# Attention products and first scores issued later, unequal gate jobs between head pairs, and memory tokens turned by VectorE and DRAM

## The chip, the cores and the metric

The kernel runs on one core of a Trainium2 chip. The metric is device time in microseconds (us), the median of several executions; lower is better. TensorE (PE) multiplies matrices and writes PSUM; VectorE (DVE), ScalarE (ACT) and GpSimd (POOL) work on tiles in SBUF and PSUM; SyncE (SP) issues DMAs, and so do ScalarE and GpSimd from their own queues.

## The reference

One layer of a streaming encoder on 512 tokens of 1024 channels in float32, with 256 memory tokens. The residual stream is normalized and fed to four parallel mixers: A, differential attention with 4 heads; F, forgetting attention with 8 heads of 64; C, a convolution module; D, a short gated convolution. Each mixer's output is projected, weighted by a gate that is itself a product of the normalized tokens, summed, and projected. Then come a cross-attention into the memory tokens and a gated feed-forward part.

```python
h = _rms_norm(x, norm_mix_pre[l])
(a_q, a_k, a_v, f_q, f_k, f_v, f_g, c_u, s_x, s_b, s_c) = jnp.split(h @ w_in[l], cuts, axis=-1)
ya = _diff_attention(...)       # softmax(q1 k1) - lam * softmax(q2 k2), chunk-causal, times v
yf = _forgetting_attention(...) # softmax(q k + c_q - c_k), causal, times v
proj = jnp.einsum('bsnc,ncd->bsnd', jnp.stack([ya, yf, yc, ys], axis=2), w_branch[l])
gates = jax.nn.sigmoid(h @ w_gate[l] + b_gate[l]).reshape(B, S, N_BRANCH, D)
x = x + _rms_norm(jnp.sum(gates * proj, axis=2) @ w_out[l], norm_mix_post[l])
m = _rms_norm(mem, norm_mem[l])
xk, xv = jnp.split(m @ w_xkv[l], 2, axis=-1)   # cross-attention's keys and values
```

## The kernel before

**Arithmetic.** Each float32 product is made of three matmuls: both operands are split into a rounded high part (a cast by ScalarE) and a rest (a subtraction by VectorE), and high x high, low x high and high x low are summed in PSUM (`split` L152 to L156, `split_weights` with the casts on L190 and L191, `matmul` L231). A projection of 128 output channels over 512 tokens is 24 matmuls of 512 columns, called a job below.

**The order of work.** `mixer_jobs` (L1143) yields the jobs of TensorE one after the other: the mixers' projections, the gates' products and the branches' products. `run_blocks` (L203) runs them and loads weights three jobs ahead. Between jobs, `bg.tick()` steps the background tasks (`Background`, L47 to L80): generators that emit the attention's scores, softmax, turning and value products. Each yields an estimated cost and a wait; a task goes on only when an estimated clock, which `matmul` and `transpose` advance, has passed the wait, and while a credit of 0.7 of that clock remains. Two tasks at most are stepped at once. A scheduler then places the emitted instructions in each engine's queue; `tc.issue_after(x)` asks it to place an instruction behind x.

**Attention.** The four heads of A (`a_task`, L860) are queued by `qk_jobs` (L769) between gate jobs of branch c, and the four pairs of heads of F (`f_task`, L1016) between gate jobs of branch a: `mixer_jobs` yields the query and key projections of pair 0, and then, for pairs 1 to 3, the pair's projections and four jobs of the generator `ga` (L1179, L1180). When a pair's keys are projected they are evacuated from PSUM into the tile `qk` (L790 to L792), and its task is queued. A task makes four groups of scores, of 128, 256, 384 and 512 keys, with softmax. The probabilities must be turned (keys on partitions) before they multiply v. There are two ways:

- "far" heads (h < 3) and pairs (p < 3): VectorE turns 32 by 32 squares (`turn_squares` L819), `put` (L822) writes the tile to DRAM from ScalarE's queue, `get` (L831) reads it back in the turned order, and `split_in_place` (L835) casts (L839) and subtracts.
- the last head and the last pair: TensorE transposes through PSUM (`to_keys_major` L804, transposes on L238), and `split` casts and subtracts.

`values` (L842) multiplies with v in two halves, after step 5 and step 7 of the far tasks (3 and 5 of the last). Accumulators of the values are emptied on L1094 and L1095 for F. PSUM banks have the tags mm, av, sc and tr, two of each.

**The memory tokens.** `mem_task` (L1238) is a background task beside the last gate's jobs (branch f): it loads two tiles of 128 memory tokens, normalizes them (`normed` L280), and `to_channels` (L292) has TensorE transpose each (8 transposes), ScalarE cast twice and VectorE subtract twice into `ns.mt`, which the products of `kx_jobs` and `vx_jobs` read after the mixers' output projection.

Of the kernel before, what the change touches and what calls it, by code (L numbers as in the profile page):

```python
# [25 lines left out]
P = 128  # L26
# [57 lines left out]
def hybrid_layer(ctx: ExitStack, tc: tile.TileContext, a: dict, out: bass.AP):  # L84
# [114 lines left out]
        return w[k0 * P:(k0 + nk) * P, c0:c0 + n].rearrange("(k p) c -> p k c", p=P), [P, nk, n]  # L199

    bg = Background(0.7, 2)

    def run_blocks(jobs, ahead=3):  # L203

# [24 lines left out]
            bg.tick()  # L229

    def matmul(ps, lhs, rhs, start, stop):  # L231
        PE.matmul(ps, lhs, rhs, start=start, stop=stop)  # L232
        bg.clock += max(int(math.prod(rhs.shape[1:])), 256) * 0.00042

    turns = []
# [56 lines left out]
    def to_channels(y_t, act, t):  # L292

        sl = slice(t * P, (t + 1) * P)
        for half in range(2):
            ps = bank("tr")
            ks = slice(half * 4, half * 4 + 4)
            for k in range(4):
                transpose(ps[:, k * P:(k + 1) * P], y_t[:, (half * 4 + k) * P:(half * 4 + k + 1) * P])
            split(ps.rearrange("p (k c) -> p k c", k=4), act[0][:, ks, sl], act[1][:, ks, sl])  # L300
# [516 lines left out]
        evacuations[:] = [ins.ins]  # L817

    def turn_squares(dst, src):  # L819
        V.transpose(dst.rearrange("p (b t i) -> p b t i", b=4, i=32), src.rearrange("p (t j b) -> p b t j", b=4, j=32))  # L820

    def put(e, w):  # L822
        d = dram.tile([2, P * S], F32, tag="turned", name="turned", bufs=6)[:e.shape[1], :P * w]
# [36 lines left out]
    def a_task(h, qk, v):  # L860
        es, pt, av = {}, None, None
        far = h < 3
        for step in range(8 if far else 6):
            if step in ((5, 7) if far else (3, 5)):
                if av is None:
                    av = bank("av")
                vh, vl = (x[:, :, h * P:(h + 1) * P] for x in v[0])
                values(av, lambda kt: ((vh[:, kt], 0), (vh[:, kt], 1), (vl[:, kt], 0)), pt, step // 2 - (2 if far else 1))
            cost = 0.0
            if far:  # L870
                for qt in SPLITS.get(step, ()):
                    split_in_place(qt + 1, pt, qt % 2)
                    cost += 0.1 + 0.15 * qt
                for qt in GETS.get(step, ()):
                    if qt % 2 == 0:
                        pt = pt_tiles()
                    get(es.pop(qt)[:, 0], qt + 1, pt, qt % 2)
            elif 1 <= step <= 4:
                if step in (1, 3):
                    pt = pt_tiles()  # L880
                to_keys_major(es.pop(step - 1)[:, 0], step, pt, (step - 1) % 2)
                cost += 0.1 + 0.15 * step
            if step < 4:
                qt, w = step, (step + 1) * P
                e = es[qt] = e4()
                st = m1p.tile([P, 8], F32, tag="st8", name="st8", bufs=4)
                for c in range(2):
                    ps = bank("sc")
                    scores(ps, qk, c, qt * P, w)
                    V.tensor_tensor_reduce(e[:, c, :w], ps[:, :w], mask_a[:, S - w:], scale=1.0,  # L890
                                           scalar=-3.0e38, op0=ALU.add, op1=ALU.max,
                                           accum_out=st[:, c:c + 1])
                V.tensor_scalar(st[:, 2:4], st[:, 0:2], -HD ** -0.5, None, ALU.mult)
                for c in range(2):
                    A.activation(e[:, c, :w], e[:, c, :w], AF.Exp, bias=st[:, 2 + c:3 + c],
                                 scale=HD ** -0.5, accum_out=st[:, 4 + c:5 + c])
                V.reciprocal(st[:, 6:8], st[:, 4:6])
                V.tensor_scalar(st[:, 7:8], st[:, 7:8], lam, None, ALU.mult)
                A.activation(e[:, 1, :w], e[:, 1, :w], AF.Copy, scale=st[:, 7:8])
                V.scalar_tensor_tensor(e[:, 0, :w], e[:, 0, :w], st[:, 6:7], e[:, 1, :w], ALU.mult,  # L900
                                       ALU.subtract)
                cost += 0.6 + 0.0035 * w
                if far:
                    turn_squares(e[:, 1, :w], e[:, 0, :w])
                    es[qt] = put(e[:, 1:], w)
                    cost += 0.0015 * w
            if step == (7 if far else 5):
                e = e4()
                A.copy(e[:, 0], av)
            yield cost, 4.0 if far else 3.5  # L910

        ps = bank("tr")
        for t in range(NT):
            transpose(ps[:, t * P:(t + 1) * P], e[:, 0, t * P:(t + 1) * P])
        A.activation(e[:, 1], ps, AF.Square, scale=1.0 / math.sqrt(P))
        ms = m1p.tile([P, NT], F32, tag="ms4", name="ms4", bufs=2)
        V.tensor_reduce(ms, e[:, 1].rearrange("p (t c) -> p t c", t=NT), AX.X, ALU.add)
        r = rstd_of(m1p, [ms], NT)
        V.tensor_tensor(e[:, 0].rearrange("p (t c) -> p t c", t=NT),
                        ps.rearrange("p (t c) -> p t c", t=NT),  # L920
                        r.unsqueeze(2).to_broadcast([P, NT, P]), ALU.mult)
        yield 1.5, 3.5
        ps2 = bank("tr")
        for t in range(NT):
            transpose(ps2[:, t * P:(t + 1) * P], e[:, 0, t * P:(t + 1) * P])
        if "a" not in y:
            y["a"] = (y8b(), y8b())
        split(ps2, y["a"][0][:, h], y["a"][1][:, h], half["dn"])
        yield 0.6, 0.0
# [86 lines left out]
    def f_task(p, qk, v):  # L1016
# [5 lines left out]
        for j in range(2):  # L1022
            t = m1p.tile([P, S], F32, tag="ck", name="ck", bufs=2)
            G.dma_start(t, crows[2 * p + j:2 * p + j + 1, :].rearrange("a s -> (a s)").partition_broadcast(P))
            ck.append(t)
        yield 0.0, 2.0
        es, pts, av = {}, None, None
        for step in range(8 if far else 6):
            if step in ((5, 7) if far else (3, 5)):
                if av is None:  # L1030
                    av = [bank("av"), bank("av")]
                for j in range(2):
                    hl = v[0][:, :, 2 * p + j]
                    values(av[j], lambda kt: ((hl[:, kt], 0), (hl[:, kt], 1)), pts[j], step // 2 - (2 if far else 1))
            while step == (2 if far else 1) and f_steps[p - 1] < (8 if p - 1 < 3 else 6):
                yield 0.0, 0.5
            f_steps[p] = step + 1
# [19 lines left out]
            if step < 4:  # L1057
# [24 lines left out]
                if far:  # L1082
# [2 lines left out]
                        turn_squares(turned[:, j, :w], e[:, j, :w])  # L1085
                    es[qt] = put(turned, w)
                    cost += 0.003 * w
            yield cost, 4.5
        if "f" not in y:
            y["f"] = (y8(), y8())  # L1090

# [51 lines left out]
    def mixer_jobs():  # L1143
        yield from c_jobs()
        yield then(lambda: bg.add(lam_task(), "lam"))
        yield from d_jobs()
        yield then(lambda: bg.add(conv_norm_task(), "conv"))
        wide = m1p.tile([P, NT, D], F32, tag="v", name="wide")
        free = iter([wide[:, i] for i in (0, 1, 2, 3) * 2])
        ns.out_sums = out_sums = Sums(w_out, NK // 2, lambda: next(free), SP, "out_sums")  # L1150
        steps = {5: (out_sums.load, 0), 6: (out_sums.load, 1), 9: (out_sums.add, 0), 10: (out_sums.store, 0),
                 11: (out_sums.add, 1)}
        for i, job in enumerate(gate_blocks(3, "d")):
            yield job
            if i in steps:
                yield then(lambda f=steps[i]: f[0](f[1]))
        yield then(lambda: y.pop("d"))
        vj = v_jobs(O_AV, va)
        yield then(lambda: (out_sums.store(1), out_sums.load(2), out_sums.load(3)) and None)
        for f, q in ((out_sums.add, 2), (out_sums.add, 3)):  # L1160
            yield next(vj)
            yield then(lambda f=f, q=q: f(q))
            yield then(lambda q=q: out_sums.store(q))
        yield from vj
        yield share(False)
        gc = gate_blocks(2, "c")
        for h, n in enumerate((0, 2, 4, 6)):
            yield from qk_jobs(O_AQ, O_AK, h, lambda qk, h=h: bg.add(a_task(h, qk, va), "a"))
            if n:
                yield then(lambda: bg.drain("conv"))  # L1170
            for _ in range(n):
                yield next(gc)
        yield then(lambda: bg.drain("a"))
        yield from vf_jobs(vf)
        yield from kv_blocks(0)
        ga = gate_blocks(0, "a")
        for p in range(1, 4):
            yield from kv_blocks(p)
            for _ in range(4):  # L1179
                yield next(ga)  # L1180
        yield then(lambda: bg.drain("f"))

# [55 lines left out]
    def mem_task():  # L1238
        for t in range(2):
            m_t = stage("s1", "m_t")  # L1240
            G.dma_start(m_t, mem_d[t * P:(t + 1) * P, :])
            y_t = normed(ns.xm, m_t, [ns.gain], stage("s2", "mn"))
            if t == 0:
                space(ns.xm, "gap8", 96)
            yield 1.3, 8.0
            to_channels(y_t, ns.mt, t)
            yield 1.2, 0.0

    def kx_jobs():
# [577 lines left out]
```

## Time and profile before

| | before |
|---|---|
| median of 3 executions | 1061.24 us (1059.8 to 1061.26) |
| the profiled execution's own time | 1061.52 us |
| its span in the profile | 1059.7 us |
| TensorE busy | 1045.3 us, 99% |
| VectorE busy | 806.2 us, 76% |
| ScalarE busy | 499.7 us, 47% |
| GpSimd busy | 144.7 us, 14% |
| DMA | 164.37 MB, 155 GB/s mean |

All times in the profile are microseconds from the start of the span. A row of the timeline has the start, the duration, the engine, the line, the operation and its operands, and how many instructions it stands for; in square brackets stand the idle time before it and what ended that. Records of matmuls overlap: their starts are what counts. `ps_mm`, `ps_av`, `ps_sc` and `ps_tr` are PSUM banks by tag; `wh` and `wl` are the parts of a weight tile, `pth` and `ptl` of turned probabilities, `mth` and `mtl` of turned memory tokens. A row of the waits has the waiting group, the releaser, the total, how many times, and the longest. The attention of A lies at about 200 to 410 us, F's at 375 to 530, the last gate with the memory tokens at 505 to 575.

### The profile page before, as it was taken

Reading aid. Unit: us, or ns where it says so; the run is one execution under the profiler, and the core shown is the slowest. Engines: PE = TensorE matmul, PEld = TensorE weight load, DVE = VectorE, ACT = ScalarE, POOL = GpSimd, SP = SyncE. Lnnn points to the kernel's source line nnn. Section 1 sums busy time; section 2 is a strip of 40 time slices with the busy share of each in tenths; the row PEclk is TensorE's granted clock in tenths of the full one; section 3 lists DMA queues with packets and bytes.
Section 4 is the critical chain, followed back from the end, with each engine's and each line's share of the span. In section 5 each row is a group of like instructions: output and inputs, shape, how many; then the busy total and the mean of one; then the engine's idle time right before and its main releaser. Section 6 shows DMA issues by size and latency. Waiting matters only on the chain.

```text
span 1059.7 us, 14521 instructions
## 1 busy us (share of the span) xinstructions
PE 1045.3 (99%) x5279; PEld 886.9 (84%) x5279; DVE 806.2 (76%) x1277; ACT 499.7 (47%) x820; POOL 144.7 (14%) x246
## 2 busy tenths in 40 slices
PE   9999999999999999999999999999999999999997
PEld 7888888888888987887878899999888888888886
DVE  6999997568677368787676888886768677667796
ACT  5322222367555355644543665654333333445672
POOL 4000000000000014322110031031111211111001
PEclk9999999999999999999999999999999999999999
DMA  7954333324333245565335743226576676725662
GB/s 260 314 159 96 108 89 100 99 83 141 115 103 108 56 124 173 170 189 145 100 113 177 268 137 119 81 79 193 185 247 214 215 230 213 232 80 179 211 217 79
DMA packets 186109, 164.37 MB, mean 155 GB/s; under 512 B 20352, under 2 KB 158061, under 8 KB 186038
## 3 DMA queue, kind: packets, MB, share of 16 engines
q1 hardware_dynamic: 152995, 119.91, 37.4%
q10 hardware_dynamic: 30482, 35.01, 10.0%
q0 software_dynamic: 2560, 8.54, 2.5%
q8 instruction: 41, 0.67, 0.3%
q14 instruction: 31, 0.25, 0.1%
HBM read 139.69 MB, written 23.74 MB: 154 GB/s over the span
## 4 chain that ended last, share of the span: by engine, by line
PE 89%; issue 4%; DVE 4%; DMA 2%; ACT 1%; POOL 0%; ACTq 0%; SPq 0%; POOLq 0%; DVEq 0%
PE ps_mm L232 46%; PE ps_av L232 29%; PE ps_sc L232 7%; PE ps_tr L232 4%; PE ps_tr L238 2%; DVE wl L191 1%; DMA e<-in_w_in 1%; PE ps_mm L450 1%; PE ps_av L450 1%; DVE e L820 0%; DVE e L1071 0%; ACT e L1076 0%; DMA ck<-crows 0%; DVE e L890 0%; DVE qk L792 0%
## 5 line engine op out<-in xcount | busy, mean ns | idle before, releaser
L190 ACT CAST wh<-wr 128x1024 fp32r<-128x1024 f32 (+1 forms) x140 | 146.7, 1049 | 271.1 <-PE ps_mm L232 154.2
L191 DVE TENSOR_TENSOR wl<-wr,wh 128x1024 fp32r<-128x1024 f32 (+1 forms) x140 | 175.6, 1255 | 104.9 <-ACT wh L190 104.8
L232 PE MATMUL ps_mm<-hth,wh 128*128 128x512 f32 (+1 forms) x616 | 231.0, 381 | 1.0 <-DVE qk L792 0.9
L232 PE MATMUL ps_mm<-htl,wh 128*128 128x512 f32 (+1 forms) x616 | 229.7, 379 | 0.0
L232 PE MATMUL ps_mm<-hth,wl 128*128 128x512 f32 (+1 forms) x616 | 229.4, 379 | 0.0
L232 PEld LDWEIGHTS ps_mm<-hth,wh 128*128 128x128 f32 x616 | 114.3, 188 | 22.4 <-PE ps_sc L232 1.4
L232 PEld LDWEIGHTS ps_mm<-hth,wl 128*128 128x128 f32 x616 | 113.9, 188 | 21.5
L232 PEld LDWEIGHTS ps_mm<-htl,wh 128*128 128x128 f32 x616 | 114.2, 188 | 20.3
L232 PE MATMUL ps_av<-htl,wh 128*128 128x512 f32 (+1 forms) x328 | 122.6, 374 | 0.0
L232 PE MATMUL ps_av<-hth,wh 128*128 128x512 f32 (+1 forms) x328 | 122.5, 374 | 0.0
L232 PE MATMUL ps_av<-hth,wl 128*128 128x512 f32 (+1 forms) x328 | 122.5, 374 | 0.0
L682 DVE SCALAR_TENSOR_TENSOR y<-y,par,y 128x508 f32<-128x508 f32 (+29 forms) x120 | 83.1, 736 | 0.1
L232 PEld LDWEIGHTS ps_av<-hth,wl 128*128 128x128 f32 x328 | 61.7, 188 | 11.0
L232 PEld LDWEIGHTS ps_av<-htl,wh 128*128 128x128 f32 x328 | 61.5, 188 | 10.9
L232 PEld LDWEIGHTS ps_av<-hth,wh 128*128 128x128 f32 x328 | 61.6, 188 | 10.7
L1618 DVE TENSOR_TENSOR wl<-dw,wh 128x1024 fp32r<-128x1024 f32 x32 | 40.1, 1258 | 15.0 <-ACT wh L1617 14.8
L1617 ACT CAST wh<-dw 128x1024 fp32r<-128x1024 f32 x32 | 33.5, 1052 | 22.4 <-PE ps_tr L232 7.9
L1565 ACT ACTIVATE th<-c 128x512 f32<-128x512 f32 x22 | 13.9, 632 | 48.9 <-DVE c L612 48.9
L1065 POOL TENSOR_SCALAR fbias<-ck,cq 128x128 f32<-128x128 f32 (+3 forms) x32 | 22.9, 722 | 78.0 <-DVE st L1071 72.5
L612 DVE SCALAR_TENSOR_TENSOR c<-ps_mm,par,c 128x510 f32<-128x510 f32 (+1 forms) x44 | 32.7, 744 | 0.7
L232 PE MATMUL ps_mm<-y8b,wh 128*128 128x512 f32 x96 | 30.9, 402 | 0.8 <-DVE ge L1124 0.8
L232 PE MATMUL ps_mm<-y,wh 128*128 128x512 f32 x96 | 30.5, 396 | 0.2 <-DVE ge L1124 0.2
(479 smaller groups left out, 2091.8 us busy)
## 6 DMA issues: line engine op xcount, KB each, us to landing
wr<-in_w_up SPq DMA_DIRECT2D x44, 512.0 KB
wr<-in_w_in SPq DMA_DIRECT2D x38, 512.0 KB
wr<-in_w_gate SPq DMA_DIRECT2D x32, 512.0 KB
wp<-in_w_down ACTq DMA_DIRECT2D x22, 512.0 KB
sums<-wp ACTq DMA_DIRECT2D x22, 512.0 KB
dw<-sums SPq DMA_DIRECT2D x44, 256.0 KB
wr<-in_w_branch SPq DMA_DIRECT2D x16, 512.0 KB
wide<-in_w_out SPq DMA_DIRECT2D x12, 512.0 KB
```

What stands on the lines that cost most here:

```text
L190: order(A.copy(hi, raw[:, :n]))
L191: low.tensor_tensor(lo, raw[:, :n], hi.bitcast(F32), ALU.subtract)
L232: PE.matmul(ps, lhs, rhs, start=start, stop=stop)
L238: turns.append(PE.transpose(ps, x, ident[:n, :n]).ins)
L450: keep(PE.matmul(banks[c][:, :S // 2], w[p == 1][:, k, c * P:(c + 1) * P], ht[p == 2][:, i * 4 + k, :S // 2], start=(i, p, k) == (0, 0, 0) ...
L612: ins = V.scalar_tensor_tensor(dst[:, s:], src[:, :S - s], w(k), dst[:, s:], ALU.mult, ALU.add)
L682: ins = V.scalar_tensor_tensor(dst[:, s:], src[:, :S - s], pc("conv_dw", k * 4 + j), dst[:, s:], ALU.mult, ALU.add)
L1065: G.tensor_scalar(bias[:, :w], ck[j][:, :w], -1.0, cq[:, qt, head:head + 1], ALU.mult, ALU.add)
L1565: A.activation(th, c[:, 0], AF.Silu)
L1617: A.copy(hi, x)
L1618: V.tensor_tensor(lo, x, hi.bitcast(F32), ALU.subtract)
```

## The change

- `matmul` keeps its latest instruction in `steps_of`. The value products of far heads and pairs are placed behind the latest matmul emitted before them.
- `a_task` begins with a wait of 3.0; `f_task`'s first wait is 5.0 instead of 2.0. The wait between step 5 of far tasks, which issues the last reads from DRAM, and step 6, which splits them, is 6.0 instead of 4.0 in A and 6.5 instead of 4.5 in F.
- Between the pairs of F stand 3, 4 and 5 jobs of branch a's gate instead of 4, 4 and 4.
- `mem_task` turns the normalized tokens as the far heads do: two stream transposes on VectorE for each tile, a write of the tile to DRAM and four reads from it on ScalarE's queue, then one cast and one subtraction over 1024 columns. The 16 transposes on TensorE and their casts and subtractions are gone.

```diff
     def matmul(ps, lhs, rhs, start, stop):
-        PE.matmul(ps, lhs, rhs, start=start, stop=stop)
+        steps_of[:] = [PE.matmul(ps, lhs, rhs, start=start, stop=stop).ins]
...
     def turn_squares(dst, src):
-        V.transpose(dst.rearrange("p (b t i) -> p b t i", b=4, i=32), src.rearrange("p (t j b) -> p b t j", b=4, j=32))
+        if len(dst.shape) == 2:
+            dst = dst.rearrange("p (b t i) -> p b t i", b=4, i=32)
+        V.transpose(dst, src.rearrange("p (t j b) -> p b t j", b=4, j=32))
...
     def a_task(h, qk, v):
         es, pt, av = {}, None, None
         far = h < 3
+        yield 0.0, 3.0
...
-                values(av, lambda kt: ((vh[:, kt], 0), (vh[:, kt], 1), (vl[:, kt], 0)), pt, step // 2 - (2 if far else 1))
+                with tc.issue_after(steps_of[0]) if far else ExitStack():
+                    values(av, lambda kt: ((vh[:, kt], 0), (vh[:, kt], 1), (vl[:, kt], 0)), pt,
+                           step // 2 - (2 if far else 1))
...
-            yield cost, 4.0 if far else 3.5
+            yield cost, (6.0 if step == 5 else 4.0) if far else 3.5
...
-        yield 0.0, 2.0
+        yield 0.0, 5.0
...
-                for j in range(2):
-                    hl = v[0][:, :, 2 * p + j]
-                    values(av[j], lambda kt: ((hl[:, kt], 0), (hl[:, kt], 1)), pts[j], step // 2 - (2 if far else 1))
+                with tc.issue_after(steps_of[0]) if far else ExitStack():
+                    for j in range(2):
+                        hl = v[0][:, :, 2 * p + j]
+                        values(av[j], lambda kt: ((hl[:, kt], 0), (hl[:, kt], 1)), pts[j],
+                               step // 2 - (2 if far else 1))
...
-            yield cost, 4.5
+            yield cost, 6.5 if far and step == 5 else 4.5
...
-            for _ in range(4):
+            for _ in range(2 + p):
                 yield next(ga)
...
-            yield 1.3, 8.0
-            to_channels(y_t, ns.mt, t)
+            yield 1.3, 5.0
+            for i in range(2):
+                turn_squares(m_t.rearrange("p (b t i) -> p b t i", b=4, i=32)[:, :, 4 * i:4 * i + 4],
+                             y_t[:, i * S:(i + 1) * S])
+                yield 1.0, 0.0
+            d = dram.tile([P * D], F32, tag="turned_m", name="turned_m", bufs=2)
+            A.dma_start(d.rearrange("(p x) -> p x", p=P), m_t)
+            yield 0.0, 13.0
+            hi, lo = (x[:, :, t * P:(t + 1) * P] for x in ns.mt)
+            raw = lo.bitcast(F32)
+            src = d.rearrange("(a j b k i) -> a (j b) k i", a=4, j=32, b=4, i=32)
+            for a_ in range(4):
+                with tc.issue_after(evacuations[0]):
+                    A.dma_start(raw[:, :, 32 * a_:32 * a_ + 32], src[a_])
+            yield 0.0, 8.0
+            with tc.issue_after(evacuations[0]):
+                A.copy(hi, raw)
+            V.tensor_tensor(lo, raw, hi.bitcast(F32), ALU.subtract)
             yield 1.2, 0.0
```

More of the change, by code (lines that the diff above doesn't have):

```diff
@@ L201, in hybrid_layer @@
     bg = Background(0.7, 2)
+    steps_of = []
     def run_blocks(jobs, ahead=3):
```

## The prediction

> **What bounds the kernel now.** I read the page's busy times first, then busy time by stretches, then TensorE's waits, then the timeline of the stretches in which it waits, and last the chain.
>
> ```profile
> PE 1045.3 (99%) x5279; PEld 886.9 (84%) x5279; DVE 806.2 (76%) x1277; ACT 499.7 (47%) x820; POOL 144.7 (14%) x246
> ...
> PE 89%; issue 4%; DVE 4%; DMA 2%; ACT 1%; POOL 0%; ACTq 0%; SPq 0%; POOLq 0%; DVEq 0%
> ```
> TensorE is the bound: 99% busy and 89% of the chain. An edit can shorten the run by taking matmuls away or by removing moments in which TensorE stands. Where those are, the next view tells (us; each engine's busy time; granted clock, DMA share, GB/s).
>
> ```profile
> 50.00:200.00 150.00, 150.00 (x670) 124.08 (x669) 133.63 (x194) 38.43 (x46) 6.78 (x14) 1.00 0.39 110
> ...
> 250.00:300.00 50.00, 49.21 (x245) 41.40 (x244) 37.26 (x78) 28.51 (x59) 3.47 (x6) 1.00 0.40 115
> ...
> 400.00:450.00 50.00, 48.18 (x229) 39.83 (x228) 41.83 (x94) 28.69 (x63) 19.66 (x34) 1.00 0.62 179
> 450.00:500.00 50.00, 48.02 (x221) 39.90 (x221) 38.45 (x84) 25.06 (x52) 11.88 (x22) 0.97 0.56 166
> 500.00:550.00 50.00, 49.07 (x253) 41.67 (x252) 34.49 (x67) 24.43 (x45) 8.57 (x13) 1.00 0.34 107
> ```
> From 50 to 200 us TensorE never stands. In the attention stretches it does: 0.79 us in 250 to 300, then 1.82, 1.98 and 0.93 us from 400 on, and in 450 to 500 the mean clock is 0.97. The busy column hides part of a stall, because a record lasts longer than its pitch; so I price stalls by start-to-start distances in the timeline. Who is waited for:
>
> ```profile
> PE ps_sc L232 <- DVE qk L792: 1.2, 1, 1.2
> ...
> PE ps_av L232 <- DVE e L1095: 0.9, 1, 0.9
> ...
> PE ps_av L232 <- ACT pth L839: 0.8, 1, 0.8
> ```
> These are the longest three beyond 400 us of their kinds: first scores waiting for their keys' evacuation (L792), an accumulator waiting to be emptied (L1095), value products waiting for a turned tile's cast (L839).
>
> **The change part by part.** Pitches first: 24 products of 512 columns take 5.44 us, 0.227 each; four scores of 128 columns take 0.49 us when nothing is late; and a 256-column value product 0.12 (two in 0.24).
>
> ```profile
> 40.65 5.44 PE ps_mm L232 x24
> ...
> 500.27 0.49 PE ps_sc L232 x4
> ...
> 503.48 0.24 PE ps_av L232 x2
> ```
>
> *First scores later.* Three more units of estimated clock pass before each head's scores in branch a, and each pair's in branch f. In the changed kernel's compiled order TensorE works through gate products between a pair's key projection and its first scores: for pair 3 some 25 us (summed by these pitches), where the order before leaves 3.6; for pair 2, 28 us. The keys' evacuation takes under 2 us, so these stalls go. Pair 3:
>
> ```profile
> 478.09 0.22 PE L232 MATMUL ps_sc<-qk 128*128 128x128 f32 x1
> ...
> 480.59 0.73 PE L232 MATMUL ps_mm<-y8b,wh 128*128 128x512 f32 x2 [0.81 <-DVE ge L1124]
> ```
> 2.50 us for two recorded products worth 0.25: 2.25 goes. Behind it the clock halves:
>
> ```profile
> 478.10:480.60 2.50, 0.52 (x4) 0.19 (x2) 2.50 (x7) 1.78 (x5) 2.30 (x3) 1.00 0.14 38
> ...
> 481.90:485.30 3.40, 3.40 (x11) 2.71 (x10) 3.31 (x8) 1.49 (x4) 0.48 (x1) 0.51 0.38 80
> ```
> ```profile
> 480.59 4.36 PE ps_mm L232 x12
> ```
> Twelve products take 4.36 us for 2.72: 1.64 us more, which leaves with its cause. The third head's first scores show the same:
>
> ```profile
> 265.54 0.33 PE L232 MATMUL ps_sc<-qk 128*128 128x128 f32 x2
> ...
> 266.96 0.73 PE L232 MATMUL ps_mm<-y,wh 128*128 128x512 f32 x2 [0.21 <-DVE ge L1124]
> ```
> 1.42 us for a group of four worth 0.49: 0.95 goes, since about 8 us of other products now stand in between. Two lesser groups of four (head 1, pair 1) take 0.73 and 0.71 us:
>
> ```profile
> 241.92 0.89 PE L232 MATMUL ps_sc<-qk 128*128 128x128 f32 x4
> 242.65 0.45 PE L232 MATMUL ps_mm<-hth,wh 128*128 128x512 f32 x1
> ...
> 410.70 0.88 PE L232 MATMUL ps_sc<-qk 128*128 128x128 f32 x4
> 411.41 0.68 PE L232 MATMUL ps_mm<-y8b,wh 128*128 128x512 f32 x2
> ```
> Against 0.49 that is 0.46 too much together, rounded to 0.5.
>
> *Value products later.* With the added wait and the order tied to the latest matmul, pair 1's first value products stand 31 us behind the scores that feed them, by pitches, instead of 26.
>
> ```profile
> 446.91 0.33 PE L232 MATMUL ps_av<-pth,v 128*128 128x256 f32 x1
> ...
> 449.03 0.50 PE L232 MATMUL ps_mm<-hth,wh 128*128 128x512 f32 x1
> ```
> 2.12 us for five products worth 0.47, with 0.25 for the change of tile shape as in the four scores: 1.4 goes. No instruction is added by this part; SyncE's queue only gets two weight loads in another place, and GpSimd's stays as it was.
>
> *Jobs of 3, 4, 5 between pairs instead of 4, 4, 4.* Twelve all the same, so no work changes. Pairs 2 and 3's projections move one 5.44-us job earlier, hence the 25 and 28 us above. It costs nothing while gate jobs remain as cover; the price is at the end, where the last pair, which turns its tiles on TensorE itself, has none left. In the order before:
>
> ```profile
> 525.75 1.03 PE L238 MATMUL ps_tr<-ident,e 128*128 128x128 f32 x8
> 526.54 0.48 PE L232 MATMUL ps_mm<-hth,wl 128*128 128x512 f32 x1
> ...
> 528.23 0.40 PE L232 MATMUL ps_av<-pth,v 128*128 128x256 f32 x2
> ...
> 531.16 0.73 PE L232 MATMUL ps_av<-y,wh 128*128 128x512 f32 x2 [0.93 <-DVE e L1095]
> ```
> From the transposes' start to their values 2.48 us pass, and seven products (1.59 us) cover the casts and subtractions. In the changed order the last two turned pairs stand together (3+3, then 4+4 transposes), nothing is between them and the values, and there are two transpose banks: the 4s wait until the 3s are cast (about 0.43 us each, by the x2 row of 384 columns) and subtracted:
>
> ```profile
> 520.44 0.86 ACT L155 CAST pth<-ps_tr 128x384 fp32r<-128x384 f32 x2 [0.57 <-PE ps_tr L238]
> ```
> ```profile
> 520.96 1.02 DVE L156 TENSOR_TENSOR ptl<-ps_tr,pth 128x384 fp32r<-128x384 f32 x2 [0.42 <-ACT pth L155]
> ```
> ```profile
> 519.31 1.23 DVE L191 TENSOR_TENSOR wl<-wr,wh 128x1024 fp32r<-128x1024 f32 x1 [0.40 <-ACT wh L190]
> ```
> Step by step from the first transpose: 0.33 for three, casts to 0.95, first subtraction to 1.5, the 4s from 1.6, their first cast to about 2.8, its subtraction to 3.45, where the first head's values start. TensorE has 14 transposes (1.5 us at 0.1 each) in these 3.5 us, so it stands about 2.0 us; with the second head's value a little late, 2.1. Bounds: 0 if the products behind can be had early (the order forbids it), 3.3 if a weights subtraction of 1.23 us stands first on VectorE. The wait of 0.93 us for L1095 behind it stays.
>
> The clock: 2.50 us with 0.52 busy were enough above for half clock. The new tail has two waits, 2.1 us and the 0.93 that stays, within some 5 us of short instructions. I take a second drop, +1.6; bounds 0 and 1.64. [...]
>
> Two new places in the order: branch a's products over pair 2's rows stand close behind its output's split (0.4, from 0 to 0.9, the largest accumulator wait listed), and two banks are handed on with a margin of about 0.3 us (0.3). A product's wait for qk L792 near 400 us keeps its neighbours and stays.
>
> *The memory's tokens.* Removed from TensorE: 16 transposes in two groups.
>
> ```profile
> 547.61 1.04 PE L238 MATMUL ps_tr<-ident,mn 128*128 128x128 f32 x8
> ...
> 548.72 0.40 PE L232 MATMUL ps_mm<-htl,wh 128*128 128x512 f32 x1
> ```
> 548.72 minus 547.61 is 1.11 for eight and one product of 0.23: 0.88 a group; the second group, at 558.07, is alike: 1.75 goes. [...] Added: four stream transposes on VectorE (1.1 us each by the row below) and ten DMAs on ScalarE's queue (two writes, eight reads of 128-byte pieces), while casts and subtractions become half as many of twice the width.
>
> ```profile
> L820 DVE STREAM_TRANSPOSE e<-e 128x512 f32<-128x512 f32 x9 | 9.9, 1104 | 0.0
> ```
> ```profile
> 491.38 0.93 ACTq L833 DMA_DIRECT2D ptl<-turned  x2
> ...
> 498.67 1.96 ACT L839 CAST pth<-ptl 128x384 fp32r<-128x384 f32 x4
> ```
> That is 4.4 us more on VectorE, busy 34.5 of 50 us there, and 5 us of queue on ScalarE (0.47 an issue), busy 24.4 of 50. Turned tiles read back at 491 are cast within 7.3 us; the products that read the memory's tokens stand after 600 us. Cover: gate f's products. Price if it fails: what ScalarE's blocked queue delays, up to the 0.9 us of a bank wait. I take 0.
>
> *Sum.* The profiled execution took 1061.52 us, 0.28 above the median. Minus 2.25, 1.64, 0.95, 0.5, 1.4 and 1.75 (8.5); plus 2.1, 1.6 and 0.7 (4.4): 1057.4, and against the median 1057.2.
>
> **The rivals.**
> 1. *The tail is short and keeps full clock.* For it: at 446.91 a 1-us stall left the clock whole, and the two waits at the tail are parted by values. [...]
> 2. *New waits take what the old ones gave.* Everything between 220 and 560 us is reordered, and eight stalls lay there before. If three like the ones of 0.9 us turn up where I see margins, 1057.2+2.7: 1059.9, within 0.2% (2.1 us, about what a measurement of this kernel can tell from no change).
> 3. *Slower: the last pair's softmax becomes the bound.* Its scores to its last values go from 52 us (478.09 to 530) to 33 by pitches. From the last 512-column score to the transposes the changed order leaves 8 us; the chain took 5 before, to the end of its last scaling:
>
> ```profile
> 513.94 0.63 PE L232 MATMUL ps_sc<-qk 128*128 128x512 f32 x2
> ```
> ```profile
> 518.03 0.88 DVE L1080 TENSOR_SCALAR e<-e,st 128x512 f32<-128x512 f32 x2
> ```
> If weights' subtractions of 1.23 us get between four times, that margin of 3 is gone, and beyond it each microsecond is lost; it decides from 6.2 us on, where the time passes 1063.4. Against it: VectorE has 11 idle us of 50 there.
> 4. *The tokens' turning gets in the way.* A cast that waits for a DMA holds ScalarE's queue, and weights' casts behind it. Reading at 128 bytes took under 7.3 us before, and the wait set is 13 units. Two weights jobs late by 1 us: 1059.2.
>
> **How the numbers follow.** Forecast with half clock at the tail 0.35 (1056 to 1058.5); rival 1, 0.27; rival 2, 0.17 (half of it with rival 4's few tenths on top); rival 3, 0.11; rival 4, 0.10. The range reaches from rival 1 with other small stalls gone (1053.8) to rival 2's upper end (1061.2). Faster by over 0.2% means under 1059.1: the forecast, rival 1 and most of rival 4, some of 2: 0.74. Slower, over 1063.4: 0.11. The same: 0.15.
>
> **What would show it.** No stall over 0.5 us at the first scores of pair 3 and no half clock there; 16 fewer transposes of mn; a stall of about 2 us between the last pair's transposes and its values, and the clock halved within 4 us behind it. A wait for pth L839 or qk L792 over 1 us elsewhere, or TensorE waiting for mth, would make the prediction wrong.

## The result and the profile after

The changed kernel takes 1066.48 us (median of 11 executions, 1062.07 to 1069.01) where the kernel before takes 1061.01 (11 executions, 1059.8 to 1061.89). The ratio is 1.0053 with a 95% interval of 1.004 to 1.0065: slower, by some 5.5 us, where 1057.2 was forecast. The executions also spread over 7 us instead of 2. The profiled execution took 1065.46 us with a span of 1063.7; it is 1 us under the median. Lines of the changed kernel are numbered a little higher: L1124 is now L1132, L792 is L793, L1095 is L1103, L839 is L842.

The page, busy times and chain, after:

```profile
PE 1041.7 (98%) x5263; PEld 884.3 (83%) x5263; DVE 807.9 (76%) x1279; ACT 499.2 (47%) x818; POOL 144.6 (14%) x246
...
PE 86%; DVE 4%; issue 4%; DMA 3%; ACT 1%; ACTq 1%; POOL 0%; POOLq 0%; DVEq 0%
```
TensorE has its 16 instructions fewer and is busy for 3.6 us less, and the span is still 4.0 us longer. Where that lies, the stretches tell; first those of before, then those of after (length, busy PE, PEld, DVE, ACT, POOL, granted clock, DMA share, GB/s):

```profile
200.00:550.00 350.00, 344.29 (x1752) 292.10 (x1751) 247.68 (x532) 191.31 (x372) 57.00 (x101) 1.00 0.43 125
550.00:600.00 50.00, 50.00 (x227) 41.46 (x226) 35.29 (x45) 23.33 (x29) 2.92 (x6) 1.00 0.65 220
```
```profile
200.00:550.00 350.00, 344.95 (x1761) 292.81 (x1760) 250.37 (x536) 190.06 (x369) 55.85 (x101) 1.00 0.43 126
550.00:600.00 50.00, 42.39 (x181) 34.65 (x180) 31.57 (x39) 21.05 (x24) 2.92 (x6) 0.93 0.78 229
```
The attention is a little better, with more matmuls in the same 350 us. The loss is in 550 to 600 us, which ran without a gap before: TensorE is idle for 7.6 us and its clock averages 0.93. TensorE's waits, after:

```profile
PE ps_mm L233 <- DVE ge L1132: 8.8, 2, 7.6
PE ps_mm L233 <- DVE qk L793: 1.6, 2, 1.0
...
PE ps_tr L239 <- DVE ptl L156: 1.3, 1, 1.3
...
PE ps_av L233 <- DVE e L1103: 0.6, 1, 0.6
```
L1132 multiplies a gate into its branch and so empties an mm bank. Why it was late by 7.6 us is read backwards from the timelines of TensorE, VectorE and ScalarE, and from the chain:

```profile
578.10 0.39 PE L233 MATMUL ps_mm<-wh,mix 128*128 128x512 f32 x1
586.10 0.79 PE L233 MATMUL ps_mm<-wh,mix 128*128 128x512 f32 x1 [7.61 <-DVE ge L1132]
```
```profile
574.93 1.23 DVE L156 TENSOR_TENSOR wl<-wr,wh 128x1024 fp32r<-128x1024 f32 x1 [3.44 <-ACT wh L155]
584.22 1.23 DVE L1270 TENSOR_TENSOR mtl<-mtl,mth 128x1024 fp32r<-128x1024 f32 x1 [8.06 <-ACT mth L1269]
585.36 0.68 DVE L1132 SCALAR_TENSOR_TENSOR ge<-ge,ps_mm 128x512 f32<-128x512 f32 x1
```
```profile
568.88 4.80 ACTq L1266 DMA_DIRECT2D mtl<-turned_m  x4
...
574.80 0.69 ACT L1120 ACTIVATE ge<-ps_av,s_b_gate 128x512 f32<-128x512 f32 x1
583.14 1.04 ACT L1269 CAST mth<-mtl 128x1024 fp32r<-128x1024 f32 x1 [7.66 <-DMA wide<-out_sums]
```
```profile
572.74 10.30 DMA mtl<-turned_m
```
The second token tile's four reads are issued from 568.88 on. The last one lands 10.3 us after its issue, at 583. The cast that waits for it (L1269; the releaser beside it is another load that ended at the same moment, the chain has the right one) stands next on ScalarE's queue. The subtraction (L1270) stands next on VectorE's, and behind the subtraction stands the L1132 of the bank that TensorE needs for the output projection. Its inputs had been there since about 572.4 (the last product of its branch starts at 571.98 and lasts 0.39). Behind the stall the clock falls (products start 0.43 us apart until 589.25 and 0.23 to 0.24 after it):

```profile
578.10:586.00 7.90, 0.39 (x2) 0.00 (x0) 1.78 (x2) 2.86 (x3) 0.00 (x0) 0.77 0.81 279
586.00:590.00 4.00, 3.90 (x11) 3.10 (x12) 3.90 (x7) 0.08 (x1) 0.00 (x0) 0.59 0.52 148
```
From start to start the stall is 8.00 us, less a pitch of 0.23: 7.8. At 0.59 for 4 us about 1.6 us more are lost: 9.4 in all.

### The profile page after: what moved, and what is told of

Its sections match the earlier page's. It is cut to its first block, busy times and chain, and to the rows that moved or that the text cites. A ratio compares the mean times of both kernels' runs of the same rounds, so it can differ in the third digit from the quotient of the medians.

```text
span 1063.7 us, 14500 instructions
## 1 busy us (share of the span) xinstructions
PE 1041.7 (98%) x5263; PEld 884.3 (83%) x5263; DVE 807.9 (76%) x1279; ACT 499.2 (47%) x818; POOL 144.6 (14%) x246
## 4 chain that ended last, share of the span: by engine, by line
PE 86%; DVE 4%; issue 4%; DMA 3%; ACT 1%; ACTq 1%; POOL 0%; POOLq 0%; DVEq 0%
PE ps_mm L233 45%; PE ps_av L233 27%; PE ps_sc L233 7%; PE ps_tr L233 4%; PE ps_tr L239 2%; DMA mtl<-turned_m 2%; DVE wl L191 1%; DMA ptl<-turned 1%; PE ps_mm L451 1%; PE ps_av L451 1%; DMA wr<-in_w_gate 0%; DVE ge L1132 0%; ACTq L1266 0%; DMA ck<-crows 0%; ACT e L1084 0%
## 5 line engine op out<-in xcount | busy, mean ns | idle before, releaser
L613 DVE SCALAR_TENSOR_TENSOR c<-ps_av,par,c 128x510 f32<-128x510 f32 (+1 forms) x40 | 29.8, 746 | 0.6
```

The costliest lines, as they stand in the source:

```text
L613: ins = V.scalar_tensor_tensor(dst[:, s:], src[:, :S - s], w(k), dst[:, s:], ALU.mult, ALU.add)
```

## The experiments

Each is the changed kernel with one edit, unless it says otherwise. Medians stand beside the kernel before on the same chip, with the ratio to it and its 95% interval.

**Without the token part, and with nothing else.** e1_no_mem takes the token part back; e2_mem_only is the kernel before with that part alone.

```diff
-            (the new steps of mem_task)
+            yield 1.3, 8.0
+            to_channels(y_t, ns.mt, t)
```


> The changed kernel with the memory's tokens turned by TensorE as before; all else of the change stays. Theory T (the whole loss is the turned memory tokens: 7.8 us in which TensorE waits at 578 us for the L1132 that stands behind the token subtraction on VectorE, and 1.6 us of half clock behind it): without them 1066.5 - 9.4 + 1.75 (the 16 transposes are back) = 1058.8 us, so faster than before by some 2 us. Rival R (the moved attention work costs as well, the gains seen there are illusory): 1061 to 1064 us.

> The kernel before with only the memory's tokens turned by VectorE and DRAM. T: the stall comes with that part alone, 1061.0 - 1.75 + 9.4 = 1068.7 us, with TensorE waiting 7 to 8 us for a gate's evacuation (L1124 or its line here) near 580 us. R: the stall needs the moved attention too (the last pair's end lies elsewhere), so about 1059.3 us here.

e1: 1057.46 us, before 1060.29, ratio 0.9971 (0.9959 to 0.9982). e2: 1068.06, ratio 1.0069 (1.0046 to 1.0092). The rest of the change is a gain of 2.8 us and the token part a loss of 7.8; together they make 5.0 of the 5.5 measured. In e2 the same wait is found, under that kernel's line number:

```profile
PE ps_mm L232 <- DVE ge L1126: 5.4, 3, 4.3
```
The longest wait is 4.3 us there, in an execution of 1066.72, where 7 to 8 were expected. The loss does not need the moved attention work.

**Reads issued earlier.**

```diff
-            yield 0.0, 13.0
+            yield 0.0, 5.0
```


> The changed kernel with the wait between the write and the reads of the turned tokens 5.0 instead of 13.0, so that the reads are issued some three instructions earlier on ScalarE. T1 (the second tile's reads are issued too late, and land in 6 to 10 us wherever they are): the cast no longer waits more than about 2 us, and TensorE no longer for it: 1057.1 us. T2 (the reads land late because the other queues' loads fill the DMA engines at 570 us and later, or ScalarE now waits for the write instead): a wait of 3 us or more remains, 1060 to 1064 us.

e3: 1059.45 us, ratio 0.9988 (0.9979 to 0.9996). Between the two expectations: most of the loss goes, the wait for L1132 shrinks to 2.0 us, but ScalarE's queue is now held by the reads' issue and by the write in front of them, which landed 3.80 us after its issue at 562.70:

```profile
566.52 6.06 ACTq L1266 DMA_DIRECT2D mtl<-turned_m  x4
572.70 1.05 ACT L155 CAST wh<-wr 128x1024 fp32r<-128x1024 f32 x1 [8.43 <-PE ps_mm L233]
```
Four reads of 128-byte pieces keep the queue for 6 us here.

**Larger pieces.** e5_contig reads the same bytes in 512-byte pieces, in the order in which they were written; the tokens are left in a wrong order for the products.

```diff
-            src = d.rearrange("(a j b k i) -> a (j b) k i", a=4, j=32, b=4, i=32)
+            src = d.rearrange("(p k x) -> p k x", p=P, k=NK)
...
-                    A.dma_start(raw[:, :, 32 * a_:32 * a_ + 32], src[a_])
+                    A.dma_start(raw[:, 2 * a_:2 * a_ + 2], src[:, 2 * a_:2 * a_ + 2])
```


> The changed kernel with the four reads of the turned tokens taking pieces of 512 bytes in the order in which they were written, instead of 128-byte pieces in the turned order; their number, size, place and waits stay. The tokens that the cross-attention reads are in a wrong order, so the output is left wrong. Ta (the 128-byte pieces are what makes the reads land 6 to 10 us after their issue): they land in 3 us, the wait at the end of the last gate goes, 1057 us. Tb (the loads on the other queues fill the DMA engines there, whatever the pieces): the reads still land after 580 us, and the time stays above 1063 us.

e5: 1055.85 us, before 1060.84, ratio 0.9952 (0.9938 to 0.9965). With number, bytes, queue and wait of the reads the same, the loss is gone. The issue takes 0.5 us a read, and the cast follows 4 us after the first:

```profile
566.66 0.93 ACTq L1266 DMA_DIRECT2D mtl<-turned_m  x2
...
570.69 1.05 ACT L1269 CAST mth<-mtl 128x1024 fp32r<-128x1024 f32 x1 [0.26 <-DMA mtl<-turned_m]
```
The pieces are not all that differs: the last read is issued at 568.13, before SyncE's next load at 569.65, while in the changed kernel SyncE's loads start at 570.38 in the middle of the reads. What that is worth is taken up below.

**The cast later.** Two kernels are to move the second tile's cast and subtraction behind the last gates. e6_late_cast ties them to a matmul of the output projection.

```diff
-            with tc.issue_after(evacuations[0]):
-                A.copy(hi, raw)
+        with tc.issue_after(steps_of[0]):    # after the ninth job of the output projection
+            A.copy(hi, raw)
```


> The changed kernel with the second tile's cast and subtraction issued behind a matmul in the middle of the mixers' output projection (its ninth job), where before they stood at the end of the last gate; the reads stay where they are. T (what costs is that the cast waits at the head of ScalarE's queue, and the subtraction on VectorE, in front of the gate's evacuation): TensorE's wait of 7.6 us and the half clock go, 1066.5 - 9.4 = 1057.1 us, or 1055.7 by e1_no_mem less 16 transposes. Rival (the reads' issue on ScalarE's queue, near 5 us, or the loads that they push back, hold the products too, as e3_early's 1059.45 hints): 1058.5 to 1061 us.

e6: 1066.27 us, ratio 1.005 (1.0037 to 1.0064). It says nothing on either: the tie to an instruction of another engine did not hold, and the cast even came in front of the last gate's weight cast.

```profile
584.73 1.04 ACT L1279 CAST mth<-mtl 128x1024 fp32r<-128x1024 f32 x1 [13.49 <-DMA mtl<-turned_m]
585.68 1.04 ACT L155 CAST wh<-wr 128x1024 fp32r<-128x1024 f32 x1
```
e9_late_cast2 ties them to a weight cast on ScalarE and a weight subtraction on VectorE instead.

> e6_late_cast again in a form that moves the two instructions: the second tile's cast is tied behind a cast of the output projection's weights on ScalarE, its subtraction behind one on VectorE. In the compiled order they now stand eleven instructions later on ScalarE, behind the last gates' activations and seven more weight casts. T (the loss is that the gate's evacuation stands behind cast and subtraction): the wait for L1132 goes, 1055.7 to 1057.1 us. Rival (the 128-byte reads hold back the loads of the other queues, so the weights of the output projection come too late in any case): a wait of 3 us or more near 580 us remains, 1059 to 1063 us.

e9: 1060.89 us, before 1060.93, ratio 1.0003 (0.9993 to 1.0012). Theory and rival each have a part: the wait for L1132 falls to 0.3 us and the 5.5 us by which the changed kernel is slower go, so the order behind the cast is what made the stall long. But the time stays 3.4 us above e1. New waits come up later, for ScalarE; what delays it there is not shown:

```profile
PE ps_mm L234 <- ACT hth L157: 1.3, 1, 1.3
...
PE ps_sc L234 <- ACT m L1418: 1.3, 1, 1.3
```
**1-KB pieces with everything computed.** e10_1kb_pieces lands the reads in the tile of the normalized tokens and lets the cast and the subtraction reorder; e11_1kb_late adds e9's order; e12_no_mem_again is e1 beside e11.

```diff
-            raw = lo.bitcast(F32)
-            src = d.rearrange("(a j b k i) -> a (j b) k i", a=4, j=32, b=4, i=32)
+            hi, lo = (x.rearrange("p k (a i) -> p k a i", a=4) for x in (hi, lo))
+            raw = y_t.rearrange("p (a k i) -> p k a i", a=4, i=32)
+            src = d.rearrange("(a j b x) -> a (j b) x", a=4, j=32, b=4)
...
-                    A.dma_start(raw[:, :, 32 * a_:32 * a_ + 32], src[a_])
+                    A.dma_start(y_t[:, 256 * a_:256 * a_ + 256], src[a_])
```


> The changed kernel with the turned tokens read in pieces of 1 KB (the read keeps the order in which the tile was written for each square's row, lands in the tile of the normalized tokens, and the cast and subtraction reorder). Everything is computed. Ta (the pieces' size is the cause): the cast waits under 1 us, no wait for L1132, 1055.8 us as e5_contig, which is faster than both kernels. Tb (bytes and place are): still above 1060 us.

> e10_1kb_pieces and e9_late_cast2 together: 1-KB pieces, and the second tile's cast and subtraction behind seven more weight casts. If the cast's wait of 5 us in e10 still cost something (its waits for L1132 sum to 0.9 us): 1056 us or a little under, faster than e10 (1057.2). If the mended reads already cost nothing: 1057 us, as e10 and as e12.

> e1_no_mem again, on the same chip and with the same runs of the kernel before as e11: 1057.5 us. If turning the memory's tokens off TensorE is worth the 1.75 us of its 16 transposes once its reads are mended, e11 is 1 to 2 us below this; if not, they are within 0.5 us.

e10: 1057.23 us, ratio 0.9966 (0.9953 to 0.9978): faster than both kernels, by 3.7 and 9 us, and 1.4 us above the 1055.8 expected. The issue is down to about 0.5 us a read, but the cast waits 5 us, so the 1 us expected there was wrong:

```profile
567.34 0.81 ACTq L1267 DMA_DIRECT2D mn<-turned_m  x2
568.17 1.03 ACTq L1267 DMA_DIRECT2D mn<-turned_m  x2
576.52 1.05 ACT L1270 CAST mth<-mn 128x1024 fp32r<-128x1024 f32 x1 [4.98 <-DMA mn<-turned_m]
```
The cast still starts 6.6 us earlier than in the changed kernel (583.14), and TensorE's waits for L1132 are down to 0.9 us. Of the 6.6, 4.1 come from issuing the last read earlier (568.67 instead of 572.74) and 2.5 from its landing in 7.75 us instead of 10.3.

e11: 1057.77 (0.9975, 0.9966 to 0.9985). e12: 1057.55 (0.9971, 0.996 to 0.9981). Turning the tokens off TensorE with mended reads is not measurably better than leaving its 16 transposes there. Only e5, whose reads come back sooner, shows anything of the 1.75 us. In e11 TensorE's waits sum to 8.8 us, a wait for ScalarE of 1.3 us as in e9 among them, where e12's sum to 6.8; that is about what the transposes save. Where it goes in e10 is not shown.

**The three other parts of the change**, all without the token part, against e1's 0.9971: e4_jobs444 has equal jobs, e7_no_mem_free unties the value products, e8_no_mem_soon takes the added first waits away.

```diff
-            for _ in range(2 + p):              # e4
+            for _ in range(4):
...
-                with tc.issue_after(steps_of[0]) if far else ExitStack():    # e7
+                with ExitStack():
...
-        yield 0.0, 3.0                          # e8, in a_task
-        yield 0.0, 5.0                          # e8, in f_task
+        yield 0.0, 2.0
```


> As e1_no_mem, and with 4, 4 and 4 jobs between the pairs instead of 3, 4 and 5. If the unequal jobs are worth nothing by themselves (the compiled order differs only around pair 2's start): within 0.5 us of e1_no_mem. If they carry the gain of the attention stretch: 2 us slower than e1_no_mem.

> As e1_no_mem, and the far heads' and pairs' value products are no longer tied to the latest matmul. In the compiled order pair 2's and 3's scores move up to 5 us earlier again. If the tie carries part of the gain: a wait for pth or qk of 0.5 to 2.4 us comes back, 1058.5 to 1061 us. If the added waits alone carry it: 1057.5 us, as e1_no_mem.

> As e1_no_mem, but without the added waits before the first scores (none in branch a, 2.0 in branch f). If these waits carry the gain at the first scores, as predicted: the stall of 0.95 us at the third head's first scores comes back, and something at pair 2's and 3's, 1058.5 to 1061 us. If the tied value products alone hold the first scores back: 1057.5 us, as e1_no_mem (the compiled order leaves pair 3's first scores where they are).

e4: 1058.18 us, 0.9979 (0.997 to 0.9988). e7: 1058.04, 0.9972 (0.9962 to 0.9982). e8: 1061.82, 1.0014 (1.0005 to 1.0022). The equal jobs cost 0.7 us by the medians, within the intervals; the tie of the value products is worth nothing that is seen. Without the added first waits the gain is gone: the time is 4.4 us longer than e1, and TensorE's waits sum to 9.7 us instead of 5.2.

```profile
PE ps_mm L233 <- DVE qk L793: 2.8, 3, 1.6
PE ps_mm L233 <- DVE v L156: 1.4, 1, 1.4
...
PE ps_sc L233 <- ACT qk L792: 0.6, 1, 0.6
```
The first two rows are waits for an mm bank that an evacuation of keys or values has yet to empty. First scores that wait for their keys make up only 0.8 us (0.6 and 0.2).

## Why the prediction was wrong

The forecast was 4.0 us faster; 5.5 us slower was measured. By its steps:

- *The memory's tokens: the step that failed.* It said minus 1.75 for the transposes and "I take 0" for the turning, with "up to the 0.9 us of a bank wait" if the cover fails. The transposes did go. The turning cost 7.8 us net of them (e2). Three things were wrong. The rows that priced the reads were of another kind: the four reads at 491 are of the third and fourth groups, which `get` reads in pieces of 384 and 512 bytes (128 for each tile of keys), 512 pieces a read. From 490.5 to 499 us, before, these are 2048 of the packets:

```profile
q10 hardware_dynamic: 2112, 0.92, 39.8%
```
  A read of the tokens has 1024 pieces of 128 bytes. At "0.47 an issue" ten DMAs were to take 5 us of ScalarE's queue; the eight reads alone took 10.6, with the 4.80 above and these of the first tile:

```profile
547.93 5.80 ACTq L1266 DMA_DIRECT2D mtl<-turned_m  x4
```
  Next, "Turned tiles read back at 491 are cast within 7.3 us" was taken as time enough, because the products that read the tokens stand after 600 us. But the reader that counted is the cast, the third instruction behind the reads on ScalarE, not the product. And the price was bounded by a wait that the trace happened to have, which is no bound here: the L1132 behind the cast and the subtraction waited until the DMA had landed, at 583, 10.3 us after its issue. Rival 4 named this mechanism, with 0.10 and with 1059.2, two weights jobs late by 1 us each; the place (the last gate's L1132 and not a weight) and the size (7.6 us and 1.6 of half clock) were missed.
- *First scores later: right in its result, its cause only in part shown.* No wait of a pair's first scores for its keys is left in the list of after. e8 shows the added waits' part for the third head, where this comes back, of the 0.95 us forecast (0.93 by its rows):

```profile
266.17 0.30 PE L233 MATMUL ps_sc<-qk 128*128 128x128 f32 x1 [0.58 <-ACT qk L792]
```
  Pair 3's stall and its half clock, the largest term (2.25 and 1.64), stay away in e4, e7 and e8 alike, so which of the three parts removes them is not shown. In the stretch where the clock fell it is now whole:

```profile
450.00:500.00 50.00, 49.98 (x247) 42.20 (x246) 41.19 (x93) 25.61 (x55) 13.85 (x26) 1.00 0.56 163
```
- *Value products later: half right.* The stall at pair 1's first value products is gone, but e7 has it gone without the tie too. The longer wait before the split is left as its cause; no run takes that wait out alone.
- *The tail: right in size, partly by luck.* From the first transpose to the first value 3.49 us pass, for the 3.45 of the steps. Less 14 transposes at 0.11 (0.88 for eight) that is 1.95, and with the next value 0.5 late 2.4 us, for the 2.1 that were forecast:

```profile
521.22 0.84 PE L239 MATMUL ps_tr<-ident,e 128*128 128x128 f32 x6
523.38 1.12 PE L239 MATMUL ps_tr<-ident,e 128*128 128x128 f32 x8 [1.32 <-DVE ptl L156]
524.71 0.87 PE L233 MATMUL ps_av<-pth,v 128*128 128x256 f32 x2 [0.21 <-ACT pth L155]
```
  But the second group of transposes came at 2.16 us and not at 1.6, for a weights subtraction of 1.23 us stood first on VectorE (521.63), and the first value then waited for its cast alone, not for the subtraction.
- *The half clock behind the tail: wrong.* The clock stayed at 1.00, 1.6 us better than forecast:

```profile
500.00:550.00 50.00, 47.80 (x236) 39.79 (x235) 34.02 (x61) 22.44 (x39) 4.34 (x9) 1.00 0.39 118
```
  The second drop was the author's estimate from the fall at pair 3's first scores before the change, to 0.51 behind 2.50 us with 0.52 busy. Here the clock stayed whole behind 3.49 us with 1.96 busy (the tail, 521.22 to 524.71) and fell to 0.59 behind the 7.61 us gap at 578. Which stalls bring it down, these three places don't show.
- *New waits in the attention: undersized.* Forecast 0.7, found 1.75. After 128- and 384-column scores stand two that weren't there:

```profile
413.43 0.50 PE L233 MATMUL ps_mm<-hth,wh 128*128 128x512 f32 x1 [1.16 <-DVE ge L1132]
...
432.76 0.47 PE L233 MATMUL ps_mm<-hth,wh 128*128 128x512 f32 x1 [0.59 <-DVE qk L793]
```
For the attention parts alone the sum gave 8.5 - 1.75 - 4.4 = 2.3 us of gain; e1 and e12 have 2.8 and 3.3. The total held, but partly by luck: 1.6 too much for the clock stands against some 1.05 too little for the new waits and 0.3 for the tail.

What stands beside the reads in their 10 us can be read from four traces side by side. With larger pieces the issue on ScalarE's queue is short, about 0.5 us a read, and the loss goes (e5, e10). In the changed kernel's stretch from 568 to 584 us the reads' queue (q10) moved 0.52 MB in 4160 packets, with 94.9% of the DMA engines' time taken (q1 has SyncE's loads, q0 GpSimd's):

```profile
q1 hardware_dynamic: 2142, 2.52, 45.7%
q0 software_dynamic: 432, 1.57, 28.2%
q10 hardware_dynamic: 4160, 0.52, 21.0%
```
The reads take a fifth of the engines' time there (21.0%), so it is not their own bytes that take 10 us; the loads of the other two queues took 73.9% of it. e3 has the same 128-byte pieces with SyncE's next load only at 575.04. From 571 to 576 us q1 moves nothing there:

```profile
q10 hardware_dynamic: 3214, 0.40, 51.9%
q0 software_dynamic: 50, 0.14, 7.1%
```
The last read is issued at 570.42, and the cast that needs it starts at 575.19 with no idle time before it: 4.8 us at most, where beside SyncE's loads it was 10.3. In e5 the last read, in 512-byte pieces and ahead of SyncE's load at 569.65, was back 2.5 us after its issue. In e10, in 1-KB pieces and among nine of SyncE's loads issued from 567 to 577 us (q1 took 57.1% of the engines' time there), it took 7.75 us:

```profile
568.67 7.75 DMA mn<-turned_m
```
By these figures the loads beside the reads cost more here than small pieces do, and a short issue also helps because the reads get ahead of them. The four places differ in other ways too, and no run varies the other loads alone, so this is argued and not shown; by what mechanism the other loads would delay the reads is not shown either.

## What to carry to other kernels

When work moves from the bound engine to a DMA, follow the first instruction that waits for that DMA, on its own engine's queue, and price what stands behind it by the DMA's whole landing time at that place, not by the waits that the profile has so far. Here the landing time went with the stretch: of the same 128-byte reads the last was back in at most 4.8 us with little beside it (e3) and took 10.3 among SyncE's loads. Before a price is taken from rows of another transfer, its piece size has to be the same. Where such a move stays, larger pieces are worth a reordering in the cast (e10, 9 us against the changed kernel), though here that came out level with leaving the transposes on TensorE.

## What the runs showed that was not expected

The issue of a DMA was not a fixed cost of its queue here: one of these reads, of 128 KB each, held ScalarE's queue for 0.40 to 0.52 us in 512-byte or 1-KB pieces (e5 and e10, means of the rows), and for 0.55 to 2.54 us in 128-byte pieces (the changed kernel's eight). And the kernels with this wait are unsteady: the changed kernel spreads over 7 us, e2 and e6 over 6 and 3.5, the kernel before over 2 to 3. e8, which has none of it, spreads over 3.7, so what moves is not shown.
